# Weight low parts on VectorE in the gate matrix, decay levels in one tile, rope tables moved to the feed-forward layer

## The chip, the cores and the metric

One Trainium2 chip, one core. The time is the device time of one execution in microseconds (us); smaller is better. The engines are TensorE (PE), VectorE (DVE), ScalarE (ACT), GpSimd (POOL) and SyncE (SP, which issues the DMAs); each runs its own instructions in order.

## The reference

Two blocks work on x of 512 tokens by 1024 features, all in fp32.

```
# first block
h = h + concat(conv_a, conv_b, spatial_gate)(rmsnorm(h) @ w_in) @ w_out
h = h + peer(rmsnorm(h))        # 8 heads, top 16 of 128 x 128 experts
h = h + (p @ w_pe) * sigmoid(rmsnorm(h) @ w_pg)
# second block, two layers, each with modulated norms
y = gla(h)                      # layer 0: gated linear attention, 4 heads
y = mla(h, cos, sin)            # layer 1: latent attention with rope, 8 heads
x = x + g1 * y ; x = x + g2 * swiglu(modulate(x))
```

In peer every token has 128 pairs (expert, gate); expert e = e1 * 128 + e2. In gla, log_a = log_sigmoid(low @ w_gate + b) / 16 with low = h @ w_lr of 16 columns, and inside a chunk of 64 tokens attn[i, j] = sum over k of q[i, k] k[j, k] exp(b[i, k] - b[j, k]) for j <= i, where b is the running sum of log_a. In mla the tables are sin and cos of positions * inv_freq.

## The kernel before

Activations lie transposed: a tile has 128 features as partitions and 512 tokens as columns, eight tiles for x. An fp32 product is made from three fp32r matmuls, high x high, low x high and high x low (`mm3`, lines 233 to 235). A weight block of 16 units of 128x128 comes by one DMA; `load_split` (lines 210 to 218) rounds it into wh on ScalarE (line 216) and subtracts into wl on POOL (line 217), 128x1024 at a time. `Stream` fetches and splits the blocks in order.

The first block's peer layer has three parts. `route` finds the 16 best pairs of each head; expert projections (`fill`, from `spills` and `up`) run on PE between its steps. `build_g` (line 850 on) then makes the dense gate matrix: for 8 tokens at a time DVE compares a row of column numbers with e1 and e2 (o1, o2; lines 878, 879) and multiplies o2 with the high and the low f16 part of the gates (og, line 883); PE multiplies o1 with og, sixteen 128x128 f16 matmuls per step into two `gg` banks of PSUM (line 902), and ScalarE copies them out (line 906). 64 such steps are interleaved with 35 expert projections of 24 matmuls each. Then the experts' down projections run.

`normed` (line 377) writes a norm's low parts, of every second tile on POOL. In the GLA layer, the low-rank product and the fp32 gate matmuls (line 1152) give log_a; scans give b; then each head's `gla_decay` goes through levels of halves 32, 16, 8, 4, 2, 1: for each, d = exp of the difference to the half's edge (lines 1226 to 1228), ql = q * d on DVE (1230), kl = k * d on POOL (1231), scores on PE (1244), and DVE puts the level's masked part into the head's matrix h (1247, 1249). Projections of v and r fill PE between the steps. Then comes a feed-forward layer (`ffn_`, a projection followed by `evict` on DVE and ScalarE), then MLA. MLA computes the rope tables itself (`rope_tables`, lines 1319 to 1350): about twenty DVE instructions of 512 columns on yl and a Sin on ScalarE (1346), beside the norms of the latents (yh copies, line 1375; their scale ry, lines 321 to 329). Tiles named sm are small PSUM tiles, of which there are two.

The code gives priorities in program order; a scheduler orders each engine's instructions ahead of time from its own cost model, and only a few are pinned (`keep`).

## Time and profile before

| what | us |
|---|---|
| median of three runs | 3166.45 |
| lowest and highest | 3161.38, 3166.67 |
| the profiled execution's own time | 3166.64 |
| its span in the profile | 3164.8 |
| PE busy | 3055.7 (97%) |
| DVE busy | 1870.4 (59%) |
| POOL busy | 1422.5 (45%) |
| ACT busy | 1063.8 (34%) |

The mean granted clock of TensorE is 0.986 of full speed. Busy time of a matmul includes its pipelined end, so that matmuls that follow each other at 0.227 us have durations of 0.39; what matters for PE is the distance between starts. An engine's idle time counts where the chain of work to the end runs through it.

### The profile page before, as it was taken

To read this page: it belongs to the slowest core of one execution; us is meant where nothing else is said; L and a number is where in the kernel's file an instruction comes from. 1 tells how busy PE (TensorE), PEld (TensorE's weight loads), DVE (VectorE), ACT (ScalarE), POOL (GpSimd) and SP (SyncE) were. 2 spreads that over 40 slices of the span, in tenths; PEclk is the share of its full clock that TensorE was granted. 3 is DMA by queue.
4 is the path that set the end of the run, shared out by engine and by line. 5 is a ranking of instruction groups with operands and counts; after the bars stand their busy time and mean duration, and the time that the engine had idled before them with its cause. 6 is when DMAs were issued, how large, how long until landed. Compare 5 with 4: busy or idle time off the path is not lost.

```text
span 3164.8 us, 39156 instructions
## 1 busy us (share of the span) xinstructions
PE 3055.7 (97%) x15521; PEld 2551.1 (81%) x15521; DVE 1870.4 (59%) x3266; ACT 1063.8 (34%) x1684; POOL 1422.5 (45%) x755
## 2 busy tenths in 40 slices
PE   8999999999999999999999988899999999999998
PEld 7887887777788888878888777778888887888887
DVE  8656778888677777775555566766211277552123
ACT  5432223444322223222222344343222244442222
POOL 4345666333454445444444443423544431234444
PEclk9999999999999999999999999999999999999999
DMA  4122334565765665565555221111223221122321
GB/s 156 67 94 107 120 121 147 205 239 228 269 221 200 212 207 199 204 233 201 187 187 179 86 80 62 54 41 67 98 95 107 88 76 38 61 87 82 112 89 65
DMA packets 131926, 424.89 MB, mean 134 GB/s; under 512 B 7824, under 2 KB 73872, under 8 KB 97184
## 3 DMA queue, kind: packets, MB, share of 16 engines
q1 hardware_dynamic: 131744, 422.40, 37.6%
q8 instruction: 122, 2.00, 0.2%
q14 instruction: 60, 0.49, 0.0%
HBM read 367.84 MB, written 54.53 MB: 133 GB/s over the span
## 4 chain that ended last, share of the span: by engine, by line
PE 47%; DVE 5%; ACT 1%; issue 1%; POOL 1%; DMA 0%; DVEq 0%; POOLq 0%; SPq 0%; ACTq 0%
PE mm L233 15%; PE mm L234 15%; PE mm L235 15%; DVE l L380 1%; PE sm L1244 1%; PE sm L1280 1%; DVE sq L297 0%; DVE m L371 0%; PE gg L1307 0%; PE sm L307 0%; PE gg L1301 0%; DVE x L1021 0%; PE mm L1436 0%; POOL wl L217 0%; POOL kl L1231 0%
## 5 line engine op out<-in xcount | busy, mean ns | idle before, releaser
L217 POOL TENSOR_TENSOR wl<-raw,wh 128x1024 fp32r<-128x1024 f32 (+4 forms) x526 | 1272.1, 2441 | 1587.0 <-ACT wh L216 1579.8
L233 PE MATMUL mm<-h,wh 128*128 128x512 f32 (+1 forms) x2524 | 958.5, 380 | 21.8 <-DVE x L1021 7.5
L235 PE MATMUL mm<-h,wl 128*128 128x512 f32 (+1 forms) x2524 | 948.3, 377 | 4.7 <-POOL wl L217 4.7
L234 PE MATMUL mm<-l,wh 128*128 128x512 f32 (+1 forms) x2428 | 922.0, 380 | 4.4 <-DVE l L380 4.0
L216 ACT CAST wh<-raw 128x1024 fp32r<-128x1024 f32 (+4 forms) x526 | 509.9, 996 | 961.3 <-issue 540.8
L233 PEld LDWEIGHTS mm<-h,wh 128*128 128x128 f32 x2524 | 480.1, 190 | 108.2 <-DVE x L1021 8.7
L235 PEld LDWEIGHTS mm<-h,wl 128*128 128x128 f32 x2524 | 479.4, 190 | 92.8 <-POOL wl L217 7.2
L234 PEld LDWEIGHTS mm<-l,wh 128*128 128x128 f32 x2428 | 462.1, 190 | 87.5 <-DVE l L380 5.3
L233 PE MATMUL mm<-ah,wh 128*128 128x512 f32 x1024 | 399.4, 390 | 5.1 <-DVE x L681 5.1
L234 PE MATMUL mm<-al,wh 128*128 128x512 f32 x1024 | 399.1, 390 | 0.0
L235 PE MATMUL mm<-ah,wl 128*128 128x512 f32 x1024 | 399.0, 390 | 0.0
L983 DVE CUSTOM_DVE_ANT_0 aw<-aw,c 128x1024 f32<-128x1024 f32 x96 | 206.8, 2156 | 108.0 <-DMA aw<-in_ada_w 85.4
L681 DVE TENSOR_TENSOR x<-x,mm 128x512 f32<-128x512 f32 x256 | 172.9, 681 | 147.9 <-PE mm L235 147.9
L233 PEld LDWEIGHTS mm<-ah,wh 128*128 128x128 f32 x1024 | 192.6, 188 | 46.7 <-DVE x L681 4.2
L235 PEld LDWEIGHTS mm<-ah,wl 128*128 128x128 f32 x1024 | 192.6, 188 | 40.0
L234 PEld LDWEIGHTS mm<-al,wh 128*128 128x128 f32 x1024 | 192.6, 188 | 39.9
L1529 DVE TENSOR_TENSOR sg<-sg,mm 128x512 f32<-128x512 f32 (+1 forms) x48 | 30.9, 643 | 301.2 <-PE mm L235 288.1
L670 ACT CAST ah<-a 128x512 fp32r<-128x512 f32 x128 | 79.3, 621 | 332.4 <-DVE a L668 200.6
L1021 DVE SCALAR_TENSOR_TENSOR x<-mm,mod,x 128x256 f32<-128x256 f32 (+1 forms) x112 | 66.5, 595 | 188.5 <-PE mm L235 188.4
L668 DVE TENSOR_TENSOR a<-a,g 128x512 f32<-128x512 f32 x128 | 140.0, 1120 | 60.4 <-DMA a<-act_d 46.4
L671 DVE TENSOR_TENSOR al<-a,ah 128x512 fp32r<-128x512 f32 x128 | 141.2, 1109 | 40.7 <-ACT ah L670 39.5
L233 PE MATMUL mm<-g,wh 128*128 128x512 f32 (+1 forms) x416 | 148.6, 357 | 0.0
(403 smaller groups left out, 3772.9 us busy)
## 6 DMA issues: line engine op xcount, KB each, us to landing
raw<-in_expert_u SPq DMA_DIRECT2D x64, 1024.0 KB, 5.1
raw<-in_expert_v SPq DMA_DIRECT2D x64, 1024.0 KB, 5.2
aw<-in_ada_w SPq DMA_DIRECT2D x96, 512.0 KB, 4.6
raw<-in_ffn_w_in SPq DMA_DIRECT2D x44, 1024.0 KB, 4.8
g_d<-gs SPq DMA_DIRECT2D x16, 2048.0 KB, 8.4
g<-g_d SPq DMA_DIRECT2D x32, 1024.0 KB, 6.4
act_d<-a SPq DMA_DIRECT2D x18, 1024.0 KB, 4.5
a<-act_d SPq DMA_DIRECT2D x18, 1024.0 KB, 4.8
```

Source lines behind the costliest of these rows:

```text
L216: self.keep(nc.scalar.copy(h[:, c], raw[:, c]))
L217: nc.gpsimd.tensor_tensor(lo[:, c], raw[:, c], h[:, c].bitcast(F32), ALU.subtract)
L233: nc.tensor.matmul(out, w[0], x[0], start=start, stop=False)
L234: nc.tensor.matmul(out, w[0], x[1], start=False, stop=False)
L235: nc.tensor.matmul(out, w[1], x[0], start=False, stop=stop)
L380: nc.vector.scalar_tensor_tensor(lo[:, c], t, sh(k), h[:, c].bitcast(F32), ALU.add, ALU.subtract)
L668: nc.vector.tensor_tensor(v3(a), v3(a), g4[:, :, j, :], ALU.mult)
L670: nc.scalar.copy(h, a)
L671: nc.vector.tensor_tensor(lo, a, h.bitcast(F32), ALU.subtract)
L681: nc.vector.tensor_tensor(X[n], X[n], p, ALU.add)
L983: nc.vector.tensor_tensor_reduce(w, w, c, 1.0, 0.0, ALU.mult, ALU.add, self.mod[:, i : i + 1])
L1021: self.nc.vector.scalar_tensor_tensor(x, p, self.mod[:, o + n : o + n + 1], x, ALU.mult, ALU.add)
```

## The change

Five things are changed together.

- `Stream` has an engine for its low parts. While `build_g` runs, the expert weights are split by DVE instead of POOL, and a block is split right after the last projection that precedes it. `normed` in its form without shift has all low parts on DVE.
- In `build_g` the two comparisons become one on a tile with both columns (oh, 2048 elements), the gates and their products lie beside each other in one tile too; both have two buffers.
- In GLA the low-rank weight is stored three times side by side (80 rows: 0 to 15, 32 to 47, 64 to 79), the gate weight likewise, and the second copy of the weight and the third of the activation hold low parts, so that one fp32r matmul a head (80 rows) gives what the fp32 one gave.
- `gla_decay` keeps one tile d a level: the later half holds q * exp, the earlier half k * exp, both products on DVE; the scores are d with itself, and only the later halves' rows are copied. The scores without decay come first. The last qk projection stands before the decay steps; v and r projections are cut into smaller pieces between the steps.
- `rope_tables` is a generator that runs, in pieces of 128 columns, after the evictions of the first feed-forward layer. In MLA, the eviction of latent 5 moves behind the start of the query norm, and the second head's k and q projections move ahead of the loop.

```diff
+            eng.tensor_tensor(lo[:, c], raw[:, c], h[:, c].bitcast(F32), ALU.subtract)
...
-                    eng = nc.gpsimd if k % 2 else nc.vector
-                    eng.tensor_tensor(lo[:, c], t, h[:, c].bitcast(F32), ALU.subtract)
+                    nc.vector.tensor_tensor(lo[:, c], t, h[:, c].bitcast(F32), ALU.subtract)
...
+                    if us.eng is nc.vector:
+                        us.block((gr * GE + j + 1) * KD // UB)
...
+                us.eng = nc.vector
                 self.build_g(pb, e1T, e2T, gT, g_d, fill)
+            us.eng = nc.gpsimd
...
+            for i, src in enumerate(two):
+                nc.vector.tensor_copy(d[:, :, i, :], src[:, :, None].to_broadcast([P, S, DUP]))
...
-            oh = lambda tag, bufs: pb.tile([P, TB, P], F16, tag=tag, name=self.nm(tag), bufs=bufs)
-            o1, o2 = oh("o1", 2), oh("o2", 1)
-            nc.vector.tensor_tensor(v4(o1), io4, bc(k1, t0), ALU.is_equal)
-            nc.vector.tensor_tensor(v4(o2), io4, bc(k2, t0), ALU.is_equal)
-            og = []
-            for part in parts:
-                og.append(oh("og", 4))
-                nc.vector.tensor_tensor(v4(og[-1]), v4(o2), bc(part, t0), ALU.mult)
-            return o1, og
+            oh, og = (pb.tile([P, TB, 2, P], F16, tag=t, name=self.nm(t), bufs=2) for t in ("oh", "og"))
+            nc.vector.tensor_tensor(v4(oh), io4, bc(keys, t0), ALU.is_equal)
+            for i in range(2):
+                nc.vector.tensor_tensor(
+                    og[:, :, i, :].rearrange("p t (k d) -> p t k d", d=DUP),
+                    oh[:, :, 1, :].rearrange("p t (k d) -> p t k d", d=DUP),
+                    gates[:, t0 : t0 + TB, i, None, :].to_broadcast([P, TB, P // DUP, DUP]), ALU.mult,
+                )
+            return oh, og
...
-        wg, rm = self.e("v", 8), self.e("v", 8)
-        nc.sync.dma_start(wg[:16], self.A["gla_w_gate"])
-        wl, wlh, wll = self.e("o", 4), self.e("o", 4, F32R), self.e("o", 4, F32R)
-        nc.sync.dma_start(wl[:, :P], self.A["gla_w_lr"])
-        nc.scalar.copy(wlh[:, :P], wl[:, :P])
-        nc.vector.tensor_tensor(wll[:, :P], wl[:, :P], wlh[:, :P].bitcast(F32), ALU.subtract)
+        wg, wgs, rm = self.e("v", 8), self.e("v", 8, F32R), self.e("v", 8)
+        nc.sync.dma_start(wg[:RG], self.A["gla_w_gate"])
+        nc.scalar.copy(wgs[:RG], wg[:RG])
+        lo = slice(32, 48)
+        nc.vector.tensor_tensor(wgs[lo], wg[lo], wgs[lo].bitcast(F32), ALU.subtract)
+        wl, wlh, wll = (gl.tile([P, KD, RG], dt, tag=t, name=t) for t, dt in (("lr", F32), ("lrh", F32R), ("lrl", F32R)))
+        nc.sync.dma_start(wl, self.A["gla_w_lr"])
+        nc.scalar.copy(wlh, wl)
+        nc.vector.tensor_tensor(wll, wl, wlh.bitcast(F32), ALU.subtract)
...
+            nc.scalar.copy(glr[:RG, sl], z)
+            nc.vector.tensor_tensor(glr[lo, sl], z[lo], glr[lo, sl].bitcast(F32), ALU.subtract)
...
-            nc.tensor.matmul(z, wg[:16, h * P : (h + 1) * P], glr[:16], start=True, stop=True)
+            nc.tensor.matmul(z, wgs[:RG, h * P : (h + 1) * P], glr[:RG], start=True, stop=True)
...
+            ref = b4[:, :, 0, None, s - 1 : s].to_broadcast([P, n, 2, s])
+            nc.vector.tensor_tensor(d4, b4, ref, ALU.subtract)
+            for i in range(2):
+                nc.scalar.activation(d4[:, :, i, :], d4[:, :, i, :], AF.Exp, scale=(2 * i - 1) / 16)
+            for i, x in enumerate((kh, qh)):
+                nc.vector.tensor_tensor(d4[:, :, i, :], d4[:, :, i, :], c4(x, s)[:, :, i, :], ALU.mult)
+            return d
...
+        nxt = level(LEVELS[0])
+        p = scores(kh, qh)
+        eye = masks[:, len(LEVELS), None, :].to_broadcast([P, NT, P])
+        nc.vector.tensor_tensor(
+            at.rearrange("p (t i) -> p t i", t=NT), p.rearrange("p (t i) -> p t i", t=NT), eye, ALU.mult
+        )
+        yield
+        for li, s in enumerate(LEVELS):
+            d = nxt
+            if li + 1 < len(LEVELS):
+                nxt = level(LEVELS[li + 1])
+                yield
+            p = scores(d, d)
+            four = lambda a: a.rearrange("p (t n two s) -> p t n two s", t=NT, two=2, s=s)[:, :, :, 1, :]
+            mk = masks[:, li, :].rearrange("p (n two s) -> p n two s", two=2, s=s)[:, None, :, 1, :]
+            mk = mk.to_broadcast([P, NT, P // (2 * s), s])
+            nc.vector.copy_predicated(four(at), mk.bitcast(U32), four(p))
...
-        run(steps)
-        evict(5, self.proj(st, 5 * KD, pre.hs))
         cq = new(3)
         lq = [lat[2], lat[3], lat[4]]
+        run(steps)
         steps = self.norm(lq, 384, lambda rb: self.normed(lq, lambda k: self.col("mla_g_q", k), rb, cq))
+        next(steps)
+        evict(5, self.proj(st, 5 * KD, pre.hs))
...
+        k_nope(1)
         q_rope(0)
         q_nope(0)
+        q_nope(1)
...
+            next(aside, None)
...
-        net.ffn(X, 0, b, a)
-        b = net.modulate(X, 1, 1)
-        net.mla(X, a, b)
+        with tc.tile_pool(name="rt", bufs=1) as rt:
+            net.ffn(X, 0, b, a, net.rope_tables(rt))
+            b = net.modulate(X, 1, 1)
+            net.mla(X, a, b)
```

How the instructions stand. DVE in `build_g`, the first two steps before (o: comparisons, og: gate products, kh and kl: the gates' parts):

```order
875 L878 TENSOR_TENSOR o_4802<-io,k_4794 128x1024
876 L879 TENSOR_TENSOR o_4803<-io,k_4796 128x1024
877 L878 TENSOR_TENSOR o_4810<-io,k_4794 128x1024
878 L883 TENSOR_TENSOR og_4806<-o_4803,kh 128x1024
879 L883 TENSOR_TENSOR og_4808<-o_4803,kl 128x1024
880 L879 TENSOR_TENSOR o_4811<-io,k_4796 128x1024
881 L883 TENSOR_TENSOR og_4814<-o_4811,kh 128x1024
882 L883 TENSOR_TENSOR og_4816<-o_4811,kl 128x1024
```

and now (oh: merged comparisons, kk: both keys, kg: both gates, wl: a weight's low part):

```order
884 L883 TENSOR_TENSOR oh_4800<-io,kk 128x2048
885 L883 TENSOR_TENSOR oh_4805<-io,kk 128x2048
886 L885 TENSOR_TENSOR og_4801<-oh_4800,kg 128x8x128 x2
887 L885 TENSOR_TENSOR og_4806<-oh_4805,kg 128x8x128 x2
888 L883 TENSOR_TENSOR oh_4865<-io,kk 128x2048
889 L219 TENSOR_TENSOR wl_5001<-raw_4998,wh_5000 128x1024
890 L885 TENSOR_TENSOR og_4866<-oh_4865,kg 128x8x128 x2
891 L883 TENSOR_TENSOR oh_4890<-io,kk 128x2048
892 L219 TENSOR_TENSOR wl_5001<-raw_4998,wh_5000 128x1024
893 L885 TENSOR_TENSOR og_4891<-oh_4890,kg 128x8x128 x2
```

The comparisons of a step are one row, and the subtractions that POOL made stand between the steps on DVE.

DVE at the first GLA head before (h_15747: the running sum b, h_15554: q; v: log_a, d: decay):

```order
1996 L1163 TENSOR_TENSOR v_15766<-v_15766,h_15765 128x512
1997 L1226 TENSOR_TENSOR d_15848<-h_15747 128x8x32
1998 L1164 SCALAR_TENSOR_TENSOR h_15765<-v_15343,v_15766 128x512
1999 L1227 TENSOR_TENSOR d_15848<-h_15747 128x8x32
2000 L1230 TENSOR_TENSOR ql_15852<-h_15554,d_15848 128x512
2001 L1226 TENSOR_TENSOR d_15856<-h_15747 128x16x16
2002 L1227 TENSOR_TENSOR d_15856<-h_15747 128x16x16
2003 L1230 TENSOR_TENSOR ql_15860<-h_15554,d_15856 128x512
```

and now (h_15558: b, h_15365 and h_15363: k and q; L1240: the difference, L1244: the products):

```order
1919 L1179 SCALAR_TENSOR_TENSOR h_15576<-v_15150,v_15577 128x512
1920 L1240 TENSOR_TENSOR d_15686<-h_15558 128x512
1921 L1240 TENSOR_TENSOR d_15698<-h_15558 128x512
1922 L1244 TENSOR_TENSOR d_15686<-d_15686,h_15365 128x8x32
1923 L1244 TENSOR_TENSOR d_15686<-d_15686,h_15363 128x8x32
1924 L1244 TENSOR_TENSOR d_15698<-d_15698,h_15365 128x16x16
1925 L1244 TENSOR_TENSOR d_15698<-d_15698,h_15363 128x16x16
1926 L1240 TENSOR_TENSOR d_15731<-h_15558 128x512
1927 L1240 TENSOR_TENSOR d_15743<-h_15558 128x512
1928 L1244 TENSOR_TENSOR d_15731<-d_15731,h_15365 128x32x8
1929 L1244 TENSOR_TENSOR d_15731<-d_15731,h_15363 128x32x8
1930 L1244 TENSOR_TENSOR d_15743<-d_15743,h_15365 128x64x4
```

The two products of a level are both DVE's, two levels follow each other, and all four heads' scans stand ahead of them; the undecayed scores (L1257) are taken after the fourth level.

ScalarE in MLA, around the Sin, before (yl: the rope angle, yh: latents, sq: their squares, h: a norm's high part):

```order
1234 L379 ACTIVATE h_19976<-m_20320,mod 128x256
1235 L216 CAST wh_20526<-raw_20524 128x1024 x2
1236 L1346 ACTIVATE sn<-yl_20488 128x512
1237 L1347 ACTIVATE yl_20491<-yl_20488 128x512
1238 L1375 COPY yh_20360<-mm_20368 128x256
1239 L1375 COPY yh_20362<-mm_20369 128x256
1240 L1375 COPY yh_20364<-mm_20370 128x256
```

and now:

```order
1232 L380 ACTIVATE h_19828<-m_20170,mod 128x256
1233 L380 ACTIVATE h_19830<-m_20174,mod 128x256
1234 L218 CAST wh_20349<-raw_20347 128x1024 x2
1235 L1401 COPY yh_20214<-mm_20222 128x256
1236 L1401 COPY yh_20216<-mm_20223 128x256
1237 L293 ACTIVATE sq_20335<-yh_20214 128x256
1238 L1401 COPY yh_20218<-mm_20224 128x256
1239 L1401 COPY yh_20220<-mm_20225 128x256
```

The Sin is gone from between the weight cast and the yh copies, and the copies of one half follow the cast.

## Rows read from the trace of the kernel before

**Rows 1.** busy us of each engine (instructions) in stretches, clock, DMA share, GB/s.

```profile
540.00:870.00 330.00, 318.40 (x2076) 257.65 (x2076) 271.11 (x295) 137.63 (x222) 123.90 (x45) 0.99 0.63 234
...
2190.00:2560.00 370.00, 365.96 (x1800) 310.52 (x1801) 99.64 (x151) 106.00 (x155) 167.31 (x72) 1.00 0.27 95
```

**Rows 2.** the same for PE alone in windows at half clock.

```profile
535.40:542.20 6.80, 5.88 (x25) 0.50 0.42 154
...
2020.20:2030.40 10.20, 9.87 (x22) 0.50 0.29 104
...
2590.30:2597.10 6.80, 5.90 (x14) 0.50 0.18 76
2631.20:2641.40 10.20, 10.13 (x23) 0.50 0.28 103
```

**Rows 3.** waits of PE (total us, times, longest), 515:540 and 540:853.

```profile
PE gg L902 <- DVE og L883: 4.0, 1, 4.0
PE sm L835 <- DVE e1f L826: 2.5, 1, 2.5
...
PE gg L902 <- DVE og L883: 8.6, 24, 0.6
```

**Rows 4.** instruction groups: whole page, then DVE in 540:853.

```profile
L217 POOL TENSOR_TENSOR wl<-raw,wh 128x1024 fp32r<-128x1024 f32 (+4 forms) x526 | 1272.1, 2441 | 1587.0 <-ACT wh L216 1579.8
...
L878 DVE TENSOR_TENSOR o<-io,k 128x1024 f16<-128x1024 f16 x61 | 76.9, 1261 | 2.7 <-PE gg L902 2.7
...
L883 DVE TENSOR_TENSOR og<-o,kh 128x1024 f16<-128x1024 f16 x62 | 42.8, 690 | 25.4 <-PE gg L902 23.3
```

**Rows 5.** timeline of PE near 590 (start, us, row, idle before it).

```profile
588.66 0.39 PE L235 MATMUL mm<-h,wl 128*128 128x512 f32 x1
588.89 1.07 PE L902 MATMUL gg<-og,o 128*128 128x128 f16 x16
...
590.55 0.23 PE L902 MATMUL gg<-og,o 128*128 128x128 f16 x1 [0.31 <-DVE og L883]
591.15 1.00 PE L902 MATMUL gg<-og,o 128*128 128x128 f16 x15 [0.37 <-DVE og L883]
```

**Rows 6.** timeline of DVE, then POOL, at the head of build_g.

```profile
515.39 2.85 DVE L818 TENSOR_TENSOR vals<-vals,gr 128x512 f32<-128x512 f32 x1
...
523.64 1.22 DVE L865 COPY k<-T 128x2048 f16<-128x2048 f16 x1
...
533.55 2.71 DVE L883 TENSOR_TENSOR og<-o,kh 128x1024 f16<-128x1024 f16 x1
...
527.09 8.63 POOL L217 TENSOR_TENSOR wl<-raw,wh 128x1024 fp32r<-128x1024 f32 x2 [5.66 <-ACT wh L216]
```

**Rows 7.** waits of PE, 185 to 215.

```profile
PE sm L307 <- DVE sq L297: 4.4, 1, 4.4
PE mm L233 <- DVE x L442: 1.7, 1, 1.7
```

**Rows 8.** waits of PE, gate matmuls, one DVE line; 1900 to 2075.

```profile
PE sm L1244 <- POOL kl L1231: 6.4, 3, 4.1
...
PE sm L1244 <- DVE h L1249: 3.0, 3, 1.3
...
PE sm L233 <- ACT o L1091: 0.3, 1, 0.3
...
L1152 PE MATMUL sm<-v,v 16*128 16x512 f32 x8 | 4.2, 626 | 0.0
...
L1227 DVE TENSOR_TENSOR d<-h x24: 392/416/2582, 1955.3 to 2086.6; 128x256 f32<-128x256 f32 x24
```

**Rows 9.** waits of PE in 2580 to 2635, then a timeline row of ScalarE.

```profile
PE mm L233 <- ACT yh L1375: 3.9, 1, 3.9
...
PE mm L235 <- DVE qnl L228: 0.3, 1, 0.3
...
2589.74 0.63 ACT L1346 ACTIVATE sn<-yl 128x512 f32<-128x512 f32 x1 [6.23 <-DVE yl L1344]
```

More of the change, by code (lines that the diff above doesn't have):

```diff
@@ L842, in top16 @@
         nc = self.nc
-        tmp = self.small(n, tag="tk")
+        tmp = self.small(n, tag="tk", bufs=2)
         nc.vector.max(v[:, 0:8], s)
@@ L1190, in after @@
             yield from chain(nxt)
-        weave([decay(0)], [qk_(7), v_(0, 0)], 2)
-        weave([decay(1)], [v_(0, 1), v_(1, 0)], 3)
-        weave([decay(2), chain(0)], [v_(1, 1), r_(0), r_(1)], 2)
-        weave([decay(3), after(0, 1)], [r_(2), r_(3)], 3)
-        weave([gate(1), chain(2)], [r_(4), r_(5)], 2)
-        weave([gate(2), chain(3)], [r_(6), r_(7)], 2)
+        weave([decay(0)], v_(0, 0), 2)
+        weave([decay(1)], v_(0, 1), 2)
+        weave([decay(2), chain(0)], v_(1, 0) + r_(0))
+        weave([decay(3), after(0, 1)], r_(1) + v_(1, 1) + r_(2))
+        weave([gate(1), chain(2)], r_(3) + r_(4))
+        weave([gate(2), chain(3)], r_(5) + r_(6) + r_(7))
         late = []
@@ L1215, in gla_decay, with level, scores @@
         last = b3[:, :, GCH - 1 : GCH]
-        def parts(li):
-            if li == len(LEVELS):
-                return qh, kh
-            s = LEVELS[li]
+        def level(s):
             n = S // (2 * s)
             b4 = c4(bh, s)
-            ref = b4[:, :, 0, s - 1 : s].to_broadcast([P, n, s])
             d = self.g(name="d")
             d4 = c4(d, s)
-            nc.vector.tensor_tensor(d4[:, :, 1, :], b4[:, :, 1, :], ref, ALU.subtract)
-            nc.vector.tensor_tensor(d4[:, :, 0, :], ref, b4[:, :, 0, :], ALU.subtract)
-            nc.scalar.activation(d, d, AF.Exp, scale=1.0 / 16)
-            ql, kl = self.e("ql", 3), self.g(name="kl")
-            nc.vector.tensor_tensor(ql, qh, d, ALU.mult)
-            nc.gpsimd.tensor_tensor(kl, kh, d, ALU.mult)
-            return ql, kl
-        nxt = parts(0)
-        yield
-        for li in range(len(LEVELS) + 1):
-            ql, kl = nxt
-            if li < len(LEVELS):
-                nxt = parts(li + 1)
-                yield
+            ref = b4[:, :, 0, None, s - 1 : s].to_broadcast([P, n, 2, s])
[5 more added lines that the diff above has]
+            return d
+        def scores(k, q):
             p = self.psm()
@@ L1243, in gla_decay @@
                 sl = slice(t * P, (t + 1) * P)
-                nc.tensor.matmul(p[:, sl], kl[:, sl], ql[:, sl], start=True, stop=True)
-            mk = masks[:, li, None, :].to_broadcast([P, NT, P])
-            if li == 0:
-                nc.vector.tensor_tensor(v3(at), v3(p), mk, ALU.mult)
-            else:
-                nc.vector.copy_predicated(v3(at), mk.bitcast(U32), v3(p))
+                nc.tensor.matmul(p[:, sl], k[:, sl], q[:, sl], start=True, stop=True)
+            return p
+        nxt = level(LEVELS[0])
[15 more added lines that the diff above has]
+            nc.vector.copy_predicated(four(at), mk.bitcast(U32), four(p))
         d = self.g(name="d")
@@ L1411, in mla_mix @@
         weave([values(0), steps])
-        kr = self.rope(lat[5], sn, cs)
+        kr = self.rope(lat[5], self.sn, self.cs)
         qr, qn, kn, ops, ys = {}, {}, {}, {}, []
@@ L1418, in q_rope @@
             nc.scalar.copy(t, p)
-            qr[h // 2] = self.rope(t, sn, cs, "qr", 2)
+            qr[h // 2] = self.rope(t, self.sn, self.cs, "qr", 2)
         def q_nope(h):
@@ L1687, in _layout @@
     A["gla_w_r"] = _blocks(_units(w[:, 2048:3072]))
-    A["gla_w_lr"] = w[:, 3072:].reshape(KD, P, 16).transpose(1, 0, 2)
-    A["gla_w_gate"] = I["gla_w_gate_2"][0]
+    thrice = np.zeros((KD, P, RG), np.float32)
+    gate = np.zeros((RG, 512), np.float32)
+    for o in (0, 32, 64):
+        thrice[:, :, o : o + 16] = w[:, 3072:].reshape(KD, P, 16)
+        gate[o : o + 16] = I["gla_w_gate_2"][0]
+    A["gla_w_lr"] = thrice.transpose(1, 0, 2)
+    A["gla_w_gate"] = gate
     A["gla_w_out"] = _blocks(_units_parts(I["gla_w_out_2"][0]))
```

139 lines of the change are left out of this document (72 added, 67 removed).

## The prediction

> **What bounds the kernel now.** I first cut the span by stage [rows 1]. TensorE (PE) is the engine at the end of every stage: 318.4 busy us of 330 while the selection matrix of the experts is built, 366 of 370 in the first feed-forward layer. So the change, which hardly takes work from PE, can win only what PE loses between matmuls. That loss has two forms. One is waiting, by releaser [rows 3, 7, 8, 9]. The other is clock: windows of 3.4, 6.8 or 10.2 us at a granted clock of 0.50, the 1.2 GHz level, each of them after such waits, in which half of the busy time is lost [rows 2]: 2.9 us at 535, 4.9 at 2020, 3.0 at 2590, 5.1 at 2631; with 2.6 at 1959 these five (first and last among those shown) lose 18.5 us in stages that the change touches. Then I looked at why the releasers were late. The recurring pattern is VectorE (DVE) against GpSimd (POOL): a DVE instruction that reads two SBUF tiles and starts while POOL runs a weight split (L217) ends only after it. The gate product og took 2.71 us, where its kind alone takes 0.69; the division of vals 2.85; POOL's two splits there took 8.63, where one is 2.44 on the mean [rows 4, 6]. Wherever POOL has less to do beside DVE, the late ends go.
>
> **Selection matrix (build_g), 516 to 800 us.** The change gives the weight splits of this stage to DVE, so POOL has nothing left that reads SBUF there, and merges the two equality tests of a step. Losses before: 2.5 us of wait for e1f [rows 3], 4.0 for the second og, and 24 short waits of 8.6 us together. The short ones cost more than their idle time, because a restart is slow: from the last matmul the sixteen 0.056-us matmuls normally follow after 0.23 us (588.66 to 588.89), but at 590.55 the first alone occupied 0.60 until the next could start at 591.15 [rows 5]; with the start delays I count 0.55 us for each, 24 x 0.55 = 13.2. Sum with the clock of 535 (2.9): 2.5 + 4.0 + 13.2 + 2.9 = 22.6 us.
> Does DVE keep up? Before, a step of 8 tokens cost DVE 1.26 + 0.73 + 1.22 + 0.69 = 3.9 us on the mean (first and last of the four lines in [rows 4]); 64 steps are 249 us. PE needs for the same 64 steps 64 x 0.9 + 35 expert projections x 24 matmuls x 0.227 = 248 us. A tie, hence the waits. After: the merged test has 2048 f16 elements; its bounds are 1.22 (the copy of as many elements, [rows 6]) and 2 x 0.69 = 1.38; I take 1.24, as the start-up is paid once. Two og products of 0.69. A 128x1024 split lies between 0.69 (as many f16 elements) and 4 x 0.416 = 1.66 (a 128x256 f32 subtraction is 0.416, [rows 8]); I take 1.2, because longer instructions pay the start once. 64 x 2.62 + 36 x 1.2 = 211 us against PE's 248, so PE bounds. What is left: at the head four repeated copies (4 x 1.22, up to 4 x 2.4 if writing in runs of four is slower), two tests and two og pairs stand between the transposes and the first product, about 13 us, with 43 matmuls (9.8 us) before it on PE: a wait of about 2 us, and it may go into the clock. **Gain 20 us** (10 to 23).
>
> **Routing norm, 185 to 215.** Every low part of this norm is now DVE's (half were POOL's). They stand in DVE's order ahead of the last residual additions and the squares, for which PE already waited 1.7 and 4.4 us [rows 7]. Four or five more of 0.42 us, of which one or two may meet a POOL split of 2.4 us: 2 to 5 us later on DVE; some of this is recovered because POOL's own low parts no longer lie between its splits. **Cost 2 us** (0 to 4).
>
> **Linear attention (GLA), 1900 to 2075.** (a) Gate: the eight fp32 matmuls occupied 4.2 us of PE [rows 8]; four fp32r ones at the pace of 0.23 are 0.9: gain 3.3. (b) The low-rank weight is 320 KB where it was 64, the gate weight 160 KB where it was 32. PE waited 0.3 for the low-rank split before [rows 8]; DMA, a cast of 640 columns and a subtraction come later by 0.7 + 0.4 + 0.5: cost 1.6 (0.8 to 4). (c) Decay levels: POOL's products kl are gone, and with them the 6.4 us that PE waited for POOL [rows 8]; the undecayed scores come first and need no decay. DVE's waits (h and d, 8.2 us in four of the nine rows whose first and last stand in [rows 8]) and the two clock windows (2.6 + 4.9) hang on the same chain. That is 6.4 + 8.2 + 7.5 + 3.3 = 25.4 within reach. But a level still goes subtraction, Exp, product, all of it now DVE's and ScalarE's. DVE has per level a subtraction of 512 (between 0.42 and 0.83, taken as 0.7), two products of 256 (0.42 each) and a copy of half the scores (0.4): 1.9 us, 3.8 for two levels; and a POOL split of 2.4 us comes with each 5.4 us of PE, so up to 1.2 more by the pattern above: 5.0 against the 4.5 us that PE has for two levels (12 matmuls of 0.227, 8 scores at no more than that). In the first two heads DVE stays 0.5 us behind six times (3 us), the first decayed scores wait some 4 us for two levels' chain after the gates, and one clock window of about 4 us remains. Net 25.4 - 1.6 - 3 - 4 - 4 = 12.8; as every one of the new waits also has a slow restart I take **11 us** (0 to 20).
> By the Trainium skill, Vector Engine (DVE) Microarchitecture Reference, section 5.2 Measured stream behaviour on trn2, a stream that hops at every 4-byte element loses some 0.65 cycle an element; levels that are split into halves hop so at the last level, where by that page its two products, subtraction and copy in four heads would cost an estimated 3 us more DVE time, and the sum would be up to 3 us later. The trace disagrees: the subtraction of halves, which hopped already, has a median of 0.416 and a smallest value of 0.392 us over all levels [rows 8], and I add nothing.
>
> **Attention (MLA), 2580 to 2645.** The rope tables go out of this stage. Before, ScalarE's Sin waited for DVE's clamped angle, whose steps met two POOL splits; four copies yh stood behind the Sin on ScalarE, idle for 6.23 us, and PE waited 3.9 for yh [rows 9]. That wait and the half clock behind it (3.0) go: 6.9 us. The other waits (six rows in all, first and last in [rows 9]: 2.4 us for ry and four of 3.3 together) and the window at 2631 (5.1) come from norm and rope chains that stay; both k_nope and q_nope projections now stand before the first scores, which covers the rope of q, but ten matmuls instead of fourteen stand between the second sums and the spread of ry. I take a third of the 3.3 and nothing else: **gain 8 us** (4 to 16).
> In the first feed-forward layer the tables cost some 70 small DVE instructions, about 15 us beside 99.6 busy of 370 [rows 1], two Sin and two table loads on ScalarE, and one DMA on SP's queue. The cover is that DVE serves one eviction per 5.4 us there; a step of ten small instructions can meet a split and take 5 us, which four PSUM buffers absorb. If they don't, four steps x 2.5 = 10 us. Taken at **0**. The smaller top-16 scratch stays in DVE's order: 0.
>
> **Sum** against the profiled execution's own 3166.64 us, 0.2 above the median of the runs: 3166.6 + 2 - 20 - 11 - 8 = 3129.6; from the median 3129.5.
>
> **Rivals.**
> Forecast, 0.60: range of its own 3114 to 3147.
> B, the GLA and MLA waits only change their releaser (low-rank DMA, DVE locked by POOL splits in two heads, two PSUM buffers for scores, spread of ry): GLA 0, MLA 3: 3166.6 + 2 - 20 - 3 = 3145.6. For it: DVE's 5.0 against 4.5 above. Against: POOL's 6.4 us do go. 0.14.
> C, build_g stays tied: a split on DVE waits in order for ScalarE's cast, with og behind it, or the strided writes are slower. It decides from 248 - 211 = 37 us in 64 steps, 0.58 us a step. Then its gain is 0: 3166.6 + 2 - 11 - 8 = 3149.6. For it: 36 splits now stand between og products. Against: a cast stands half a block ahead. 0.10.
> D, slower: the merged test and og lose the fast f16 rate in their new four-dimensional form (2.3 and 1.22 us). DVE then needs 64 x 4.74 + 43 = 346 us, 98 over PE; the stage grows by 98 - 20: 3166.6 + 2 + 78 - 19 = 3227.6. It decides from the same 0.58 us a step. Against it: the old forms with broadcasts run at 0.69. By the Trainium skill, VectorE: DVE Perf Modes, section What auto-detection actually checks, 16-bit tensors with step one keep the double rate, as the new forms have; the old rows agree with 0.69 for 1024. 0.08.
> E, B and C together, nothing to be measured: 3166.6 + 2 - 3 = 3165.6. 0.08.
>
> **How the numbers follow.** A difference under 0.2% (6.3 us) can't be told from no change here. Faster (under 3160.1): all but a trace of the forecast, B and C, tempered for sums of many small waits that often come back elsewhere: 0.80. Same: E and edges, 0.11. Slower: D and an unseen wait, 0.09. The range takes in the forecast's bounds, B, C and half of what lies towards E: 3108 to 3158.
>
> **What would show it.** Right: in 540 to 800 no wait for og beyond the head, DVE near 211 us without L217 on POOL; no wait of PE for POOL in GLA, gate matmuls under 1 us; no wait for yh. Wrong: tests over 1.4 us, og over 0.9, DVE's split waiting for ScalarE with PE behind; in GLA more than 10 us of waits for d or h; after the first feed-forward evictions waits for PSUM.

## The result, and the profile after

The changed kernel takes 3118.85 us (median of four runs, 3117.76 to 3120.73) against 3163.91 us for the kernel before in all its runs so far (3158.26 to 3166.67): a ratio of 0.986 with a 95% interval of 0.9843 to 0.9878. The forecast was 3129.5, the range 3108 to 3158. The profiled execution has a span of 3117.0 us, 47.8 less than that of before.

The busy times of the changed kernel, from its page:

```profile
PE 3035.7 (97%) x15517; PEld 2547.2 (82%) x15517; DVE 1823.2 (58%) x3308; ACT 1058.2 (34%) x1703; POOL 1270.0 (41%) x679
```

PE is still at 97%; POOL has 152 us less to do and DVE 47 us less. PE's own work shrank by 3 us only (the gates). Of the other 17 us of its 20, about 9 are clock: the granted clock was 0.50 for 88.5 us of the span before and for 71.2 us now, and half of the difference is the estimate. The rest was not split further; slow restarts after waits, which lie in busy time [rows 5], may be part of it. Where the 47.8 us lie is read from the start of the same PE instruction in both traces. The marks are the transposes of vals, the first and last matmuls of a part, and the matmuls that spread a norm's scale over the partitions (line 337 before, 339 after).

| stretch, by starts of PE instructions | before | after | change | forecast |
|---|---|---|---|---|
| start to the routing norm's spread | 208.8 | 207.1 | -1.7 | +2 |
| to the transposes of vals | 311.6 | 305.5 | -6.1 | -2.5 (e1f) |
| selection matrix, to its last gg matmul | 278.7 | 258.9 | -19.8 | -17.5 |
| expert projections down | 1008.7 | 1008.4 | -0.3 | 0 |
| to the ple norm's spread | 23.5 | 22.0 | -1.5 | 0 |
| ple, to the first spread of GLA's norm | 51.8 | 56.5 | +4.7 | 0 |
| to the second spread (low-rank weight) | 28.4 | 30.7 | +2.3 | +1.6 |
| GLA, to the feed-forward layer's spread | 291.5 | 268.9 | -22.6 | -12.6 |
| feed-forward layer with the tables | 350.2 | 350.2 | 0 | 0 |
| MLA, to the last feed-forward layer | 226.2 | 223.2 | -3.0 | -8 |
| last feed-forward layer to the end | 385.3 | 385.6 | +0.3 | 0 |

The selection matrix. The stretch from 513 to 772 us (us, busy of PE, PEld, DVE, ACT, POOL, clock, DMA share, GB/s), then its DVE groups; they answer to [rows 1] and [rows 4]:

```profile
513.00:772.00 259.00, 258.93 (x1867) 211.45 (x1866) 200.10 (x236) 116.98 (x196) 0.27 (x1) 1.00 0.60 234
```

```profile
L885 DVE TENSOR_TENSOR og<-oh,kg 128x1024 f16<-128x1024 f16 x116 | 73.4, 685 | 0.9
L883 DVE TENSOR_TENSOR oh<-io,kk 128x2048 f16<-128x2048 f16 x56 | 67.1, 1220 | 9.2 <-PE gg L908 9.2
...
L219 DVE TENSOR_TENSOR wl<-raw,wh 128x1024 fp32r<-128x1024 f32 x31 | 37.8, 1221 | 43.3 <-ACT wh L218 43.3
```

PE is busy 258.93 of 259 us at full clock, and no PE instruction in it waits for a releaser. A merged comparison takes 1.22 us, a gate product 0.69, a split 1.22 on the mean: the estimates were 1.24, 0.69 and 1.2. DVE idles 43 us in front of the splits, waiting for ScalarE's cast, and PE, which waits for nothing here, does not feel it. In the kernel before, PE idled 13.3 us between vals and the last gg matmul and was busy 6.6 us longer; the windows at half clock, one of 6.8 us at 535 and one of 3.4 at 559, account for about 4.6 of the 6.6.

GLA's waits of PE (total us, times, longest) between 1890 and 2060, for those of [rows 8], and the gate matmuls:

```profile
PE sm L1251 <- DVE h L1257: 2.7, 1, 2.7
PE sm L1285 <- DVE d L1276: 2.1, 1, 2.1
...
PE sm L1251 <- DVE d L1244: 0.7, 1, 0.7
PE sm L1251 <- DVE h L1270: 0.5, 1, 0.5
```

```profile
L1167 PE MATMUL sm<-v,v 80*128 80x512 f32 x4 | 1.4, 396 | 0.0
```

POOL is gone from the list, and four waits of 6.0 us together stand where 14.6 were. The gates are four matmuls of 1.4 us in all instead of eight of 4.2.

Two places got worse. In ple, DVE's timeline (start, us, row), then POOL's, then PE's wait:

```profile
1808.34 0.68 DVE L953 TENSOR_TENSOR part<-mm,rs 128x512 f32<-128x512 f32 x1
1809.25 4.90 DVE L378 TENSOR_TENSOR x<-m,x 128x256 fp32r<-128x256 f32 x2 [0.24 <-ACT x L377]
```

```profile
1808.99 4.88 POOL L219 TENSOR_TENSOR wl<-raw,wh 128x1024 fp32r<-128x1024 f32 x2 [8.78 <-ACT wh L218]
```

```profile
PE mm L235 <- DVE part L953: 3.8, 2, 2.7
```

Two low parts of the norm, now DVE's and taking about 0.4 us each where no split runs, start inside a pair of POOL splits and take 4.90 us; the product part behind them is late, and PE waits 3.8 us where it waited 1.0. In MLA, the same on DVE, POOL and PE:

```profile
2577.45 2.83 DVE L1384 TENSOR_TENSOR qr<-qr,cs 128x512 f32<-128x512 f32 x1
2580.21 0.68 DVE L230 TENSOR_TENSOR qnl<-mm,qnh 128x512 fp32r<-128x512 f32 x1
```

```profile
2577.22 4.47 POOL L219 TENSOR_TENSOR wl<-raw,wh 128x1024 fp32r<-128x1024 f32 x2 [16.86 <-ACT wh L218]
```

```profile
PE mm L235 <- DVE qnl L230: 3.5, 1, 3.5
```

The product of q's rope (qr) takes 2.83 us beside two splits, the low part qnl stands behind it on DVE, and PE waits 3.5 us for it, two heads' projections already done. Just before, PE also waits longer than it did for the scale ry of q's norm, 3.5 us instead of 2.4:

```profile
PE sm L339 <- DVE ry L331: 4.1, 2, 3.5
```

Behind the wait for qnl the granted clock falls to 0.50 for 13.65 us, longer than in any window of [rows 2]; behind the wait for part it falls for 3.4 us (PE alone: us, busy, clock, DMA share, GB/s):

```profile
2580.30:2593.90 13.60, 12.61 (x31) 0.50 0.22 77
```

```profile
1815.70:1819.10 3.40, 3.40 (x10) 0.50 0.64 265
1843.00:1853.20 10.20, 7.76 (x36) 0.50 0.01 2
```

The longer window in ple, of 10.2 us at 1843, lies behind another wait, which stood before too: 4.6 us for the squares of the next norm, which a window of 6.8 us followed in the kernel before.

```profile
PE sm L309 <- DVE sq L1049: 4.6, 1, 4.6
```

### The profile page after: what moved, and what is told of

The parts are those of the page before. It is cut to its first block, busy times and chain, and to the rows that moved or that the text cites. A ratio compares the mean times of both kernels' runs of the same rounds, so it can differ in the third digit from the quotient of the medians.

```text
span 3117.0 us, 39086 instructions
## 1 busy us (share of the span) xinstructions
PE 3035.7 (97%) x15517; PEld 2547.2 (82%) x15517; DVE 1823.2 (58%) x3308; ACT 1058.2 (34%) x1703; POOL 1270.0 (41%) x679
## 5 line engine op out<-in xcount | busy, mean ns | idle before, releaser
L219 POOL TENSOR_TENSOR wl<-raw,wh 128x1024 fp32r<-128x1024 f32 (+1 forms) x490 | 1167.7, 2406 | 1779.1 <-ACT wh L218 1519.7
```

Source lines behind the costliest of these rows:

```text
L219: eng.tensor_tensor(lo[:, c], raw[:, c], h[:, c].bitcast(F32), ALU.subtract)
```

## Experiments

Each kernel was run once with a profile beside the kernel before, unless said otherwise. Their times are read against 3118.9 us, and the reading goes by the stretches of the table. A stretch with the same code differed between these kernels, where half-clock windows lay differently: 206.2 to 208.6 us up to the routing norm's spread, 305.5 to 307.2 from there to vals, 54.8 to 56.5 in ple, 268.8 to 271.1 in GLA, and 1027.9 to 1032.3 from the last gg matmul to the ple norm's spread. Differences of that size in one run are not read.

**The norms' low parts back on POOL for every second tile.**

```diff
-                    nc.vector.tensor_tensor(lo[:, c], t, h[:, c].bitcast(F32), ALU.subtract)
+                    eng = nc.gpsimd if k % 2 else nc.vector
+                    eng.tensor_tensor(lo[:, c], t, h[:, c].bitcast(F32), ALU.subtract)
```

> Only the norms' low parts go back to GpSimd for every second tile (routing, ple and latent norms); all else as after the change. Theory: the 3.8 us wait for part in the ple stage came from two low parts on VectorE that met a weight split on GpSimd (4.90 us for two instructions of 0.42); with them gone the ple stage is 4 to 5 us shorter, clock windows included, and the routing norm is 2 to 3 us longer because its wait of 4.4 us for the squares is back: about 3116 us. Rival: the ple stage lost by its clock or by another order of the instructions: ple is unchanged, only the routing norm gets longer, about 3121 us.

Measured 3118.3 us. The ple stretch went from 56.5 to 51.8 us, the routing norm's from 207.1 to 208.3. The eight other kernels with all these low parts on DVE (the next eight runs) took 54.8 to 56.1 us in ple, each with waits of 3.8 us for part, so the loss there is 3 to 5 us. The wait for part in ple is back at its old size:

```profile
PE mm L235 <- DVE part L954: 1.0, 1, 1.0
```

and around the routing norm the waits of this kernel, then the one of the changed kernel, are

```profile
PE sm L309 <- DVE sq L299: 4.4, 1, 4.4
PE mm L235 <- DVE x L444: 1.7, 1, 1.7
```

```profile
PE mm L235 <- DVE x L443: 3.3, 1, 3.3
```

So the loss in ple is the meeting of DVE's low parts with POOL's splits. In the routing norm the change shortened the waits, one of 3.3 us in place of two of 6.1 together: before, two squares met a split (1.81 and 2.56 us instead of 0.41); now two low parts do (2.33 and 1.93), and the squares are on time. In the stretch this gain can't be read, since 208.3 lies among the times of the same code. The total shows neither: the transposes of vals came 3.6 us later after the spread than in the changed kernel, with a half-clock window of 6.8 us at 268.7, which the changed kernel lacks behind the same wait of 3.0 us for a split.

**The expert splits back on POOL, the merged comparisons kept.**

```diff
-                us.eng = nc.vector
                 self.build_g(pb, e1T, e2T, gT, g_d, fill)
...
```

The call that splits a block right after the last projection before it goes too.

> The weight splits of the selection matrix go back to GpSimd, the merged comparisons stay. Theory (lock of VectorE by GpSimd): the comparisons and gate products that start during a split end after it again, waits for og return, and the stretch from the transposes of vals to the last gg matmul grows from 248.6 us to 258 to 270; the e1f wait of 2.5 us before it returns too: 3131 to 3143 us. Rival: fewer and longer instructions were what VectorE needed, wherever the splits run: the stretch stays within 3 us, 3118 to 3122 us.

Measured 3142.46 us; the selection stretch 280.6 us, which is 1.9 over the kernel before, and the wait for e1f of 2.5 us is back. (The 248.6 us of this expectation and of the next run from the first gg matmul to the last, not from vals; by these marks this kernel took 268.7 and the kernel before 268.9.) PE's waits in it, then the gate products of DVE and the splits of POOL:

```profile
PE gg L903 <- DVE og L880: 13.2, 23, 2.7
```

```profile
L880 DVE TENSOR_TENSOR og<-oh,kg 128x1024 f16<-128x1024 f16 x119 | 145.4, 1263 | 2.0
...
L218 POOL TENSOR_TENSOR wl<-raw,wh 128x1024 fp32r<-128x1024 f32 x33 | 102.4, 3123 | 162.9 <-ACT wh L217 162.9
```

The gate products take 1.26 us on the mean instead of 0.69, the splits 3.12 instead of 2.4: the two engines hold each other up, as in [rows 6]. The whole gain of the stage hangs on the engine of the splits, with the earlier call that belongs to it. Fewer and longer instructions alone gave nothing.

**The comparisons as before, the splits on DVE.** The edit puts the old `hots` and `repeated` back:

```diff
-            nc.vector.tensor_tensor(v4(oh), io4, bc(keys, t0), ALU.is_equal)
+            nc.vector.tensor_tensor(v4(o1), io4, bc(k1, t0), ALU.is_equal)
+            nc.vector.tensor_tensor(v4(o2), io4, bc(k2, t0), ALU.is_equal)
...
```

> The comparisons are separate and the repeated tiles contiguous as before the change, the weight splits stay on VectorE. Theory: without GpSimd beside it VectorE needs 64 x (0.69 + 0.69 + 0.69 + 0.69) + 36 x 1.2 = 220 us, still under TensorE's 248, so the stretch from vals to the last gg matmul stays within 2 us of 248.6 and the time within 3117 to 3122 us: the merge is worth next to nothing. Rival: VectorE is near the bound and the merge carries half of the gain: the stretch grows by 8 us or more, over 3126 us.

Measured 3116.44 us; the stretch 259.0 us against 258.9. The window of 514 to 772 us in this kernel:

```profile
514.00:772.00 258.00, 257.95 (x1855) 209.49 (x1854) 206.11 (x299) 116.39 (x195) 0.23 (x1) 1.00 0.61 234
```

PE is busy to the end at full clock with DVE at 206 us of 258 (200 of 259 with the merge). The merge is worth 6 us of an engine that no one waits for, so nothing.

**The order in MLA as before, the tables still in the feed-forward layer.**

```diff
+        run(steps)
+        evict(5, self.proj(st, 5 * KD, pre.hs))
...
-        k_nope(1)
...
-        q_nope(1)
...
```

> In the attention stage the order of eviction 5 and of the second head's k and q projections goes back to that of before; the rope tables stay in the feed-forward layer. Theory: the new order put the second q low part behind the rope of q, which met a weight split (2.83 us for one product), and so made the 3.5 us wait for qnl and the 13.65 us clock window; without it the stage is 3 to 6 us shorter, 3113 to 3116 us. Rival: the split meets VectorE's rope chain in either order, and the waits for the rope of q (2.5 us before) take the place: the stage within 2 us, 3117 to 3121 us.

Measured 3114.17 us. From the spread of q's norm to the last feed-forward layer it took 163.9 us instead of 169.5; the 10 us before that spread got 1.1 us longer, so MLA as a whole took 218.7 instead of 223.2. The waits of PE in 2560 to 2600 are those of the kernel before without yh:

```profile
PE sm L339 <- DVE ry L331: 2.3, 1, 2.3
PE mm L235 <- ACT qrh L229: 1.4, 1, 1.4
PE mm L237 <- DVE qrl L230: 1.1, 1, 1.1
```

The small waits for the rope of q are back, together 2.5 us, and the one of 3.5 us is gone with half of its clock window (6.8 us instead of 13.65). Moving the second head's projections ahead of the loop gave PE more to do before the first scores, but it also put qnl behind the rope on DVE and left nothing for PE to do when that was late. The run takes back the move of latent 5's eviction too; the two moves were not tried apart.

**The gates and the low-rank product as before.**

```diff
-            nc.tensor.matmul(z, wgs[:RG, h * P : (h + 1) * P], glr[:RG], start=True, stop=True)
+            nc.tensor.matmul(z, wg[:16, h * P : (h + 1) * P], glr[:16], start=True, stop=True)
...
```

> Only the gates and the low-rank product of GLA go back (fp32 gate matmuls of 16 rows, a 16-column low-rank weight). Theory: the stretch from the spread of the first modulated norm to that of the feed-forward layer (30.7 + 268.9 us) gets 3.3 us longer by the fp32 matmuls and 1.3 us shorter by the smaller low-rank transfer: net +2 us, 3119 to 3122 us. Rival: PE waits for the gates' chain anyway (ScalarE's table loads, scans), so the matmuls' time is hidden and only the transfer counts: 1 to 2 us shorter, 3116 to 3118 us.

Measured 3120.24 us. The stretch to GLA's second spread got 1.9 us shorter (28.8 instead of 30.7), that behind it 3.0 us longer (271.9 instead of 268.9): the price of the larger weights and the gain of the fp32r gates, 1.6 and 3.3 in the forecast. Both agree with the forecast, though the same code spreads almost as far in these stretches; the gate matmuls' own rows give 2.8 (4.2 less 1.4).

**The old decay levels and their order too** (gates as in the last run):

```diff
+            ql, kl = self.e("ql", 3), self.g(name="kl")
+            nc.vector.tensor_tensor(ql, qh, d, ALU.mult)
+            nc.gpsimd.tensor_tensor(kl, kh, d, ALU.mult)
...
```

> As the run with fp32 gates, and the decay levels with their order of projections go back too (separate q and k parts, kl on GpSimd, undecayed scores last, v and r in their coarse pieces). Theory: the waits for kl, h and d (14.6 us in nine rows before) and the two half-clock windows come back: 17 to 21 us over the run with fp32 gates, 3137 to 3142 us. Rival: those waits were made by the late gates, which the lighter routing and ple do not change; the decay is worth under 8 us: 3122 to 3129 us.

Measured 3146.46 us, over the theory's range; the stretch behind the second spread 300.2 us, 28.3 over the run with fp32 gates. The largest wait is back:

```profile
PE sm L1250 <- POOL kl L1237: 6.2, 3, 3.3
```

But 28 us is more than the change can be credited with: in the kernel before, the same PE instructions in the same order took 291.5 us. The two windows, first of before, then of this run (busy of PE, PEld, DVE, ACT, POOL, then the clock):

```profile
1911.50:2203.00 291.50, 269.34 (x1495) 221.11 (x1496) 188.71 (x322) 118.50 (x188) 116.56 (x56) 0.96 0.16 58
```

```profile
1886.70:2186.90 300.20, 280.63 (x1498) 230.41 (x1499) 189.29 (x336) 118.91 (x188) 116.37 (x56) 0.92 0.16 58
```

DVE, ACT and POOL did the same work in both, but for 14 small DVE instructions at the end of the second, of the rope tables. PE idled 22.2 us before and 19.6 in this run; what differs is that it was busy 11.3 us longer, at a mean clock of 0.92 instead of 0.96: 47.8 us of the stretch ran at half clock instead of 20.5. The decay part with its order is therefore worth 20 us by the kernel before (291.5 against 271.9) and up to 28 by this run.

**The rope tables back in MLA, with its order of before.**

```diff
-            net.ffn(X, 0, b, a, net.rope_tables(rt))
+            net.ffn(X, 0, b, a)
...
+        sn, cs = self.rope_tables(ml)
...
```

> The rope tables go back into the attention stage and its order of before too; all other parts as after the change; to be read against the run with the attention order of before, 3114.2 us. Theory: the wait of 3.9 us for yh behind the Sin and its half-clock window return, 6 to 8 us in the stretch between the spread of the second norm and that of kv, and the feed-forward layer does not get shorter: 3120 to 3123 us. Rival: the tables cost as much in the feed-forward layer: within 2 us of 3114.

Measured 3120.32 us against 3114.17. The stretches of MLA up to kv's spread took 20.0 and 29.9 us instead of 18.1 and 25.5, and the feed-forward layer 350.2 in both. PE's wait is that of [rows 9]:

```profile
PE mm L235 <- ACT yh L1396: 3.9, 1, 3.9
```

So the tables' move is worth 6 us (6.3 in these two stretches, 7.6 in all of MLA), and costs nothing where they went.

**The product with k on POOL again, inside the joined level.**

```diff
-                nc.vector.tensor_tensor(d4[:, :, i, :], d4[:, :, i, :], c4(x, s)[:, :, i, :], ALU.mult)
+                (nc.vector if i else nc.gpsimd).tensor_tensor(d4[:, :, i, :], d4[:, :, i, :], c4(x, s)[:, :, i, :], ALU.mult)
```

> In the joined decay level the earlier half's product with k goes to GpSimd again (24 of 128x256 instead of 128x512), all else as after the change. Theory (VectorE and GpSimd lock each other): its products and the weight splits now queue on GpSimd, VectorE's subtractions meet them, and PE waits for d: GLA 5 to 12 us longer, 3123 to 3131 us. Rival: what helped was the order (undecayed scores first, finer filling), and VectorE, which is the busier engine in the first heads, is relieved: within 2 us or faster, 3114 to 3120 us.

Measured 3123.37 us; the stretch 272.9 us instead of 268.9, where the same code took up to 271.1. That lies between the two expectations: taking the products from POOL is worth some 2 to 4 us of the 20, and both ideas as they stood were off.

**The old order of the projections beside the joined levels.**

```diff
-        weave([decay(0)], v_(0, 0), 2)
-        weave([decay(1)], v_(0, 1), 2)
+        weave([decay(0)], [qk_(7), v_(0, 0)], 2)
+        weave([decay(1)], [v_(0, 1), v_(1, 0)], 3)
...
```

> Only the order of the projections beside the decay steps goes back (the last qk projection beside the first head, v and r in coarse pieces, the old weaving); the joined levels on VectorE with the undecayed scores first stay. To be read by the stretch from the second spread of GLA's norm to the feed-forward layer's spread: 268.9 us after the change; the old decay and order cost 27.2 us there, the k product on GpSimd alone 4.0. Theory A (the levels' arithmetic is what helped): the stretch grows by less than 8 us, under 3126 us. Theory B (the finer filling is what helped): by 15 us or more, over 3133 us.

Measured 3133.12 us; the stretch 282.7 us, 13.8 longer, a little under the 15 us of theory B and far above the bound of A. A level's scores are eight matmuls in the trace. In this kernel four levels' scores stand in a row with no projection between them (timeline of PE, with a wait inside the row):

```profile
1949.09 2.84 PE L1245 MATMUL sm<-d 128*128 128x128 f32 x24
1953.76 1.16 PE L1245 MATMUL sm<-d 128*128 128x128 f32 x8 [1.83 <-DVE h L1264]
```

and PE waits for the matrix h and the levels d:

```profile
PE sm L1245 <- DVE h L1264: 6.0, 3, 2.2
PE sm L1245 <- DVE d L1238: 3.6, 2, 3.4
```

Its window, and that of the changed kernel:

```profile
1889.50:2172.20 282.70, 267.46 (x1494) 226.06 (x1495) 171.66 (x337) 114.98 (x208) 80.07 (x32) 0.95 0.17 61
```

```profile
1889.00:2158.00 269.00, 257.29 (x1494) 218.84 (x1494) 167.30 (x337) 112.76 (x206) 79.69 (x32) 0.98 0.18 64
```

PE idles 15.2 us in the one (282.7 - 267.5) and 11.7 in the other (269.0 - 257.3), and it is busy 10.2 us longer for the same matmuls, at a clock of 0.95 instead of 0.98. Of the 13.8 us a quarter is idle time and three quarters is longer busy time at the slower clock: 27.3 us of this stretch ran at half clock, 10.2 in the other. By the two runs above, the clock alone can make 9 us of difference in this stretch for the same instructions, so one run does not fix the size.

**A kernel with three repairs** (timed in three rounds, as are the next two): the changed kernel with the MLA order of before, every second low part of the ple norm on POOL, and the low-rank weight's DMA issued first.

```diff
+                    eng = nc.gpsimd if both and k % 2 else nc.vector
...
+        nc.sync.dma_start(wl, self.A["gla_w_lr"])
         masks = gl.tile([P, len(LEVELS) + 1, P], F32, tag="masks", name="masks")
...
```

> The changed kernel with three repairs: the attention order of before (5.5 us in its run), every second low part of the ple norm on GpSimd (4.8 us in that stage), and the low-rank weight's DMA issued ahead of the masks and the gate weight. Theory: the three lie in different stages and add, and the earlier DMA takes the wait for the low-rank split (1.2 us) with its restart: 3118.9 - 5.5 - 4.8 - 1.5 = 3107 us. Rival: the clock windows that moved with them fall elsewhere, and half comes back: 3112 us or more.

Measured 3113.12 us (3110.44 to 3115.39; ratio to the kernel before 0.983, 0.9813 to 0.9846). Ple took 51.8 us as in its run. MLA took 220.3 us, 2.9 less than in the changed kernel, where the order's own run had 4.5 less (the 5.5 of the expectation left out the 1.1 us lost before q's spread). The wait for the low-rank split was 1.5 us instead of 1.2: the product comes 115 matmuls behind the norm's first spread instead of 126, so the scheduler had moved it earlier on PE along with the DMA. The rival was nearer.

**And the splits of MLA on DVE.**

```diff
+        st.eng = sv.eng = su.eng = nc.vector
```

> As the kernel with three repairs, and the attention stage's weight splits (20 of them) on VectorE, so that GpSimd reads nothing beside the norm and rope chains. Theory: the late ends in the ry and rope chains go (2.3, 1.4 and 1.1 us of waits and a half-clock window of 6.8 us): 3 to 6 us faster than the kernel with three repairs. Rival: the splits, in order on VectorE in front of the softmax and rope chains, delay those by 1.2 us each, and the stage gets longer by 2 us or more.

Measured 3108.27 us (3107.13 to 3110.08; ratio 0.9813, 0.9797 to 0.983). MLA took 216.9 us instead of 220.3; 3.1 of these 3.3 us lie before kv's spread (17.1 and 23.5 us instead of 18.1 and 25.5). The saving is as the theory had it, its list in part: the waits for ry (2.3) and for the low part of q's rope (1.1) are gone, that of 1.4 us stayed, and the half-clock window became 10.2 us instead of 6.8.

**And those of ple.**

```diff
+            st.eng = se.eng = nc.vector
```

> As the kernel with the attention stage's splits on VectorE (3108.3 us), and the ple stage's weight splits (two streams) on VectorE too. Theory: in ple the chains on VectorE (ph and pl, ry, part) lose their late ends behind GpSimd: waits of 1.3, 1.0 and 1.0 us and a half-clock window go, 2 to 5 us faster, 3103 to 3106 us. Rival: those waits come from the chain PE, VectorE, ScalarE, GpSimd, VectorE of the gated sum, which no split touches, and each split on VectorE delays a part: within 2 us or slower, 3107 to 3111 us.

Measured 3103.34 us (3100.61 to 3104.55; ratio 0.9802, 0.9785 to 0.9818), the fastest of all. The kernel before was 1.3 us faster beside this one than beside the last, and the intervals of the two ratios overlap, so the step between them is clear in the stretches rather than in the ratio. The ple stretches took 19.7 and 49.4 us instead of 22.0 and 51.4. Its splits on DVE:

```profile
L219 DVE TENSOR_TENSOR wl<-raw,wh 128x1024 fp32r<-128x1024 f32 x8 | 9.8, 1222 | 6.4 <-ACT wh L218 6.4
```

Eight splits cost DVE 9.8 us at 1.22 each, half of what they cost POOL. PE's waits for pl (1.3) and for the ple norm's ry (1.0) are gone, that for part (1.0) and the half clock stayed. Two splits of GLA's first weights, still on POOL, go on holding the next norm's chain: one of its small DVE instructions takes 2.39 us instead of 0.16.

## Why the prediction was right, and where not

The direction came out by the steps that were named. The size came out near in part by luck: two of the terms were off by more than half, with opposite signs, and one stage was left out.

- What bounds. PE with its waits and the clock behind them: right. 18.5 us of clock were counted in touched stages (two windows of 3.4 us there, at 559 and 2071, were left out), and the mechanism, DVE instructions that end only after POOL's split, is shown by putting the splits back in the selection matrix (280.6 against 258.9 us) and by taking them away in MLA and ple (3.3 and 4.4 us).
- Selection matrix. Forecast 20 with the e1f wait, measured 19.8 and the e1f wait of 2.5 us beside it. The durations were right to 2%. The term for slow restarts was too large and a clock window was missing, which offset each other: beyond the idle time 4.6 us (13.2 less 8.6) were counted for 24 restarts, and the 6.6 us of longer busy time leave an estimated 2, with the windows at 535 and 559 taken off. The wait of 2 us foreseen at the head did not come: PE waits for nothing there. That the merge of the comparisons takes part in the gain was implied by the sum for DVE, and is wrong: DVE would have had room without it. Rivals C and D had their prices (1.22 us a test, no split that holds PE) against them.
- Routing norm. Forecast a cost of 2, measured none: 206.2 to 208.6 us in twelve kernels against 208.3 and 208.8 in the two with the old low parts. The failed step is "of which one or two may meet a POOL split": two did, but the meeting was not taken off for the squares, which had met a split before and are free now; PE waits 3.3 us in all instead of 6.1.
- Between the routing norm and vals, 3.6 us more than e1f went. That is a half-clock window of 6.8 us behind a wait that stayed (the kernel of the first experiment, which has the window, is 3.6 us longer there); whether it falls there changes from kernel to kernel: of the fourteen kernels with a trace, two have a window of 6.8 us there, five one of 3.4, and seven none. That is not an effect of the change that can be planned.
- Ple. Forecast nothing, measured a loss of 4.7, and of 2.9 to 4.2 in eight other kernels with this code. The prediction costed the low parts in the routing norm only; the same line serves ple. This is the one step that was left out rather than mis-sized.
- GLA. Forecast 11, measured 20.3 (2.3 lost, 22.6 won); rival B, by which the waits only change their releaser and GLA gains nothing, is out here. Gates 3.0 and weights 1.9 were as said (3.3 and 1.6), though the sign "gate matmuls under 1 us" was missed: their busy time, which includes their ends, is 1.4. The mis-sized term is the stalls that would remain: 3 us behind DVE in the first two heads, 4 for the first decayed scores and 4 of clock, and a rounding down for slow restarts. Measured were 3.4 us for the first decayed scores (0.7 and 2.7), 2.6 for the rest, and one window of 3.4 us, 1.7 us lost: 7.7 instead of 12.8, which explains 5 of the 9 us; the other 4 are not traced to a term. What was not priced at all is the finer filling: with the old order the stretch was 13.8 us longer in the one run made, three quarters of it clock.
- The rule weighed there, on streams that hop at every 4-byte element (the Trainium skill, Vector Engine (DVE) Microarchitecture Reference, section 5.2 Measured stream behaviour on trn2), would by that estimate have made the sum up to 3 us later. The product of halves has a median of 0.413 us and a maximum of 0.427 over all levels, so nothing of it is seen there and the measurement decides; the copy of scores does show a step (below).
- MLA. Forecast 8, measured 3.0, which was rival B's figure. The move of the tables is worth 6 to 7.6, as the 6.9 for yh said, and with the order of before the stage came out 7.5 us shorter than before (218.7 against 226.2). The failed step is "both k_nope and q_nope projections now stand before the first scores, which covers the rope of q": the new order cost 4.5 us by its own run and 2.9 by the kernel with repairs, since qnl came behind the rope on DVE, and POOL's splits were at that place. The longer wait for ry that the prediction feared came too (3.5 us instead of 2.4), though q's spread came 1.1 us earlier than with the old order.
- The feed-forward layer. Forecast 0, measured 0.0 of 350.2.

Together, as measured less forecast by the table: -7.3 us up to vals, -2.3 in the selection matrix, +3.2 in ple, -9.3 in GLA, +5.0 in MLA, some tenths elsewhere. The sum is 11 us of 48: the forecast of the whole is nearer than those of its parts, because ple and MLA made up for half of what GLA and the head gave. That is luck.

## What to carry to other kernels

Where one engine's stream of large two-input subtractions runs beside another engine's chain on SBUF, look at the durations of the chain's instructions in the trace and not at busy shares: an engine at 77% that is not held up (DVE in the selection stage) cost PE nothing, and the same engine beside POOL's splits cost 20 us. Count a moved instruction at every place where its line runs. When a short wait is removed or made, price the slow clock behind it too, but as a chance: the same wait had it in one kernel and not in another.

## What the runs showed of the hardware

- The clock can be the larger part of a wait's price, and it varies. The same GLA instructions of PE took 291.5 and 300.2 us in two kernels at mean clocks of 0.96 and 0.92; a wait of 3.5 us in MLA was followed by 13.65 us at half clock, one of 2.7 for part in ple by 3.4 us, and one of 4.6 us for the squares there by 10.2 us in the changed kernel and by 6.8 in the kernel before. A wait of 3.0 us for a split at 264 us was followed by none in the changed kernel, and by 6.8 us in another.
- VectorE's 128x1024 fp32 subtraction takes 1.22 us; GpSimd's has a mean of 2.41 in the changed kernel, and 3.12 beside the gate products in the run with the splits back on POOL.
- The predicated copy of halves out of PSUM takes 0.42 to 0.45 us in the levels of 32, 16, 8 and 4, and 0.72 to 0.74 in those of 2 and 1, as long as the whole 512 elements took before (0.74); the products in place have no such step. The groups of the two lines (min, median, max in ns) in the changed kernel:

```profile
L1270 DVE COPY_PREDICATED h<-masks,sm x24: 415/436/739, 1937.7 to 2037.4; 128x256 f32<-128x256 uint32 x24
...
L1244 DVE TENSOR_TENSOR d<-d,h x48: 402/413/427, 1933.0 to 2018.9; 128x256 f32<-128x256 f32 x48
```

What makes the step, the output that hops, the source in PSUM or the mask, was not tried.
